# A four-layer decoder step on one core: two more pairs by seven products, two pairs of weight sums made later, norms and a decode store moved

## The chip, the cores and the metric

The kernel runs on one core of a Trainium2 chip. The time is the device time of one execution in microseconds (us). Three executions took 2382.0, 2383.22 and 2391.43 us, with a median of 2383.22 us. The engines are named as in the profile: PE is TensorE, DVE is VectorE, ACT is ScalarE, POOL is GpSimd, SP is SyncE. SP and POOL issue the transfers.

## The reference

The reference is one inference step of a small decoder with 1024 prompt positions, eight single-token samples and a model width of 2048. Its core, cut:

```python
def pool_layer(x, prefix, pos, w_in, w_grp, scale, w_out, g_ln, b_ln):
    z = x @ w_in
    u, gate = z[..., :D_POOL], z[..., D_POOL:]
    d, new_state = multiscale_pool(u, prefix, pos)        # trailing windows 2, 4, 8, 16
    d = jnp.einsum('btgc,gce->btge', d.reshape(B, T, N_POOL_GROUPS, POOL_GROUP), w_grp)
    d = d.reshape(B, T, D_POOL) * scale
    y = (d * jax.nn.silu(gate)) @ w_out
    return layer_norm(ALPHA * x + y, g_ln, b_ln), new_state

def attn_layer(x, pos, kb, vb, k_pos, q_pos, blocked, w_in, sinks, w_out, g_ln, b_ln):
    z = x @ w_in
    q = rope_partial(z[..., :D_ATTN].reshape(B, T, N_HEADS, HEAD_DIM), pos)
    gate = z[..., D_ATTN:]
    o = attn_core(q, kb, vb, q_pos, k_pos, sinks).reshape(B, T, D_ATTN)   # window 128, sinks
    y = (o * jax.nn.silu(gate)) @ w_out
    return layer_norm(ALPHA * x + y, g_ln, b_ln)
```

One pool layer runs first, then the shared keys and values (`w_kv`) are projected from its output, then one attention layer. Everything is float32. The matrices that matter are called `wia` (into the pool layer), `woa` (out of it), `wkv`, `wib` (queries and gates of the attention layer) and `wob` (out of it, the last matrix).

## The kernel before

**Chunks and stages.** The positions are cut into chunk 0 (512 positions) and chunk 1 (512 and the eight samples, 520). The stages stand in `PHASES`, an order written by hand: pool-layer input of chunk 0 (stage one, in a plain part and a part by seven products) and of chunk 1 (two), its output matrix for both chunks (three and four), attention input of chunk 0 (five, again in two parts) and of chunk 1 (six), and the last matrix for chunk 0 (seven) and chunk 1 (eight).

**Exact products in halves.** Each float32 operand is split into a rounded high half (a cast on ACT, L464 for weights, L742 for activations) and the rest (a difference on DVE, L479 and L751). A block of weights times a tile is then three matmuls: high by high, high by low, low by high (L631, L632, L633 in the seven-product form, L659, L660, L661 in the plain form). Every third matmul needs the difference.

**Eight or seven products.** Weights come in pairs of 128-column blocks, cut into four quarter blocks of 128 x 1024. In the plain form (`unit`) four blocks meet 512 positions each: for one pair two units of 48 matmuls with 512 columns. In the seven-product form (`pair` and `seven`, a Strassen scheme) seven blocks, three of them as they are and four of them sums, meet seven half-width tiles, three as they are and four sums: 7 x 24 = 168 matmuls with 256 (or 260) columns. The sums of activations are made by DVE (`t_ops`, L799 to L802) in a background generator (`t_gen`) and stored in `Td`. The sums of weights are made the first time that a pair is met, by `plain_pair` (L275, with its stores at L276 on POOL) or by `first_pair` (L328, stores at L329 on POOL), and loaded again by `next_pair` for the second chunk. For the output matrices a generator, `sum_gen`, makes them ahead of time: for each pair four parts of 256 columns, each with two loads at L405 (SP), three additions at L412, L416 and L417 (DVE) and a store at L418 (POOL). Then both chunks use `next_pair`.

**Stage five.** A step `p` is a pair of query blocks and a pair of gate blocks, and with them the attention of two heads pairs `t` in small matmuls between the others: scores (L1517), a transposition (L1570), values (L1594). A query is rotated before its scores (`q_done`: products at L1382, a sum at L1489, with data swapped between partitions by transfers at L1374). Before, steps 0 to 3 are plain and steps 4 to 7 go by seven products.

**Background work.** `end` runs after each block's matmuls (a plain unit has four such ends, a seven-product pair seven). It takes one step of the generator at the head of `side` whenever `int(i / every)` grows and enough slots are free, and one of `extra` (`sum_gen` of `wob`). In the plain part of stage five `side` holds the norm of chunk 1 after the pool layer (`ln_gen`, L848 to L927, whose output goes through `t_ops` as well) and the `t_gen` of chunk 0. In stage eight it holds the last norm of chunk 0 (`ln_gen`, L884 to L927). A stage that needs a generator's result forces its remaining steps (`ready`, `sums`).

**Order and memory.** PE, DVE and ACT run in the order of the source (`in_order`), so an instruction that waits holds all behind it on its engine. SP and POOL also issue in their order. Almost all tiles live in 53 slots (`Mem`), each of 1040 floats per partition, handed out by age of release. A tile that takes over a slot waits for the last readers of the one before, transfers too.

**The decode.** In stage six, after the gates of steps 3 and 7, `decode` attends the eight samples for half of the heads; its second half runs on into stage seven. Its steps `s0` to `s9` share one half slot `W`. The last, `s9` (L1735 to L1743), multiplies the values by the gate (kept in `sgd`, one tile for each half) and stores the result to `act["o", 1]` on SP (L1741).

Of the kernel before, what the change touches and what calls it, by code (L numbers as in the profile page):

```python
# [47 lines left out]
N_CST = 384 + 4 * NST  # L48

PHASES = (  # L50
    ("ai", 0, (0, 1)), ("ai", 0, (1, 4)), ("ai", 1, (0, 4)), ("ao", 0, None), ("ao", 1, None), ("bi", 0, (0, 4)),
    ("bi", 0, (4, 8)), ("bi", 1, (0, 8)), ("bo", 0, None), ("bo", 1, None),
)
PHASE_OF = {"x": "ai", "g": "ao", "h": "bi", "o": "bo"}
INPUT_OF = {k: x for x, k in PHASE_OF.items()}
# [13 lines left out]
    (5, 0), (5, 2), (5, 1), (6, 0), (5, 3), (5, 4), (6, 2), (6, 1), (7, 0), (6, 3), (7, 2), (7, 1), (6, 4),  # L69
    (7, 3), (7, 4), (5, 5), (5, 6), (6, 5), (6, 6), (7, 5), (7, 6),  # L70
)
X_KEEP = 5
X_AGE = 3
SIDE_KEEP = 5
# [105 lines left out]
class Kern:  # L180
# [174 lines left out]
    def build_stream(self):  # L355
        io = self.io
        w = []
        for kind, c, part in PHASES:
            seven, locked = (kind, c, part) not in PLAIN, (kind, c) in LOCKED
            pr = (lambda name, q: self.next_pairs(name, [q], False)) if seven else self.plain_pair  # L360
            if seven and c == 0:
                pr = lambda name, q: (lambda f: [f[i] for i in ORDER7])(self.first_pair(name, q))
            if kind == "ai":
                for g in range(*part):
                    for q in (2 * g, 2 * g + 1, 8 + 2 * g, 9 + 2 * g):
                        w += pr("wia", q)
                    for h in range(2):
                        w.append(self.lone(io["wg"][g][:, h * 1024 : (h + 1) * 1024]))
            elif kind == "bi":
                if part[0] == 0:  # L370
                    w += self.next_pairs("wkv", range(2), locked) if seven else pr("wkv", 0) + pr("wkv", 1)
                if seven:
                    for p in range(*part):
                        w += pr("wib", p) + pr("wib", 8 + p)
                else:
                    for p in range(*part):
                        q, g = pr("wib", p), pr("wib", 8 + p)
                        w += q[:2] + g[:2] + q[2:] + g[2:]
            else:
                name = "woa" if kind == "ao" else "wob"  # L380
                if (kind, c, part) != PHASES[-1]:
                    w += self.next_pairs(name, range(8), locked)
                    continue
                w += self.next_pairs(name, range(SPLIT[0]), locked)
                late = {q: self.next_pair(name, q) for q in SPLIT}
                w += [late[q][i] for q, i in TAIL]
        self.stream = w
        self.loaded = self.made = self.cast = self.prepped = 0
        self.hl, self.late = {}, []

    def sum_gen(self, name):


        W = 256
        parts = [(q, slice(W * h, W * h + W)) for q in range(8) for h in range(4)]
        w = self.io[name]
        held = {}

# [8 lines left out]
        def add(n):  # L407
            q, cs = parts[n]
            s = held[n]
            t = s.v(4, W)  # L410
            add = self.nc.vector.tensor_add
            add(t[:, 0:2, :], t[:, 0:2, :], t[:, 1:3, :])  # L412
            if name == "wob" and self.hurry is not name:
                yield
            held.pop(n)
            add(t[:, 2, :], t[:, 2, :], t[:, 0, :])  # L416
            add(t[:, 3, :], t[:, 3, :], t[:, 2, :])  # L417
            self.nc.gpsimd.dma_start(self.ws[name][q][:, :, cs], t)  # L418
            s.free(True)
            if n % 4 == 3:  # L420
                self.summed[name] = q + 1

        if name == "wob":

# [1232 lines left out]
    def decode(self, c, pr):  # L1657
# [4 lines left out]
        x = {}  # L1662
# [70 lines left out]
                    )  # L1733

        def s9():  # L1735
            a3 = a[:, :64].rearrange("p (t b) -> p t b", t=8)
            nc.vector.scalar_tensor_tensor(
                a3, x["p"][:, :64].rearrange("p (b t) -> p t b", t=8), 0.5, self.sgd[pr][:],
                op0=ALU.mult, op1=ALU.mult,
            )  # L1740
            nc.sync.dma_start(self.act["o", c][:, 8 * pr : 8 * pr + 8, TP:], a3)  # L1741
            x["v"].free(True)
            W.free()  # L1743

        for n, go in zip(DEC_AT[pr], (s0, s1, s2, s3, s4, s5, s6, s7, s8, s9)):
# [109 lines left out]
    def run(self):  # L1855
# [15 lines left out]
        for n, (kind, c, part) in enumerate(PHASES):  # L1871
# [36 lines left out]
            elif (kind, c) == ("bi", 0) and not self.strassen:  # L1908
                self.summed["wob"] = 0
                self.extra = self.sum_gen("wob")  # L1910
                for k in (4, 40):
                    self.at(k, lambda k=k: setattr(self, "on", k == 4))
                add(("h", 1, False), self.ln_gen(1, *acc[1], C_GA, C_BA, self.act["h", 1], self.Td.get(("h", 1))))
                add(("h", 0, False), self.t_gen(("h", 0)))

                for k in range(10):
                    self.at(2 * k + 3, lambda: self.side and self.lastO < self.i - 1 and self.side_step())
                self.every = 1.2
            elif (kind, c) == ("bi", 1):
                self.at(8, lambda: setattr(self, "on", True))  # L1920
                self.every, self.room = 1, 0
            elif (kind, c) == ("bo", 0):
                self.at(23, lambda: setattr(self, "ahead", (7, 4, 3)))
                self.at(18, lambda: add(("o", 1, False), self.t_gen(("o", 1))))
                self.at(16, lambda: [s.free() for s in self.kv])
                self.rt.free()
            elif (kind, c) == ("bo", 1):
                gen = self.ln_gen(0, *acc[0], C_GB, C_BB, io["y0"], None)
                self.at(3, lambda gen=gen: add("y", gen))
                self.every = 2  # L1930
            if kind == "ai":
                self.phase_ai(c, range(*part), nxt)
            elif kind == "bi":
# [149 lines left out]
```

## Time and profile before

| what | value |
| --- | --- |
| median of three runs | 2383.22 us |
| profiled execution, its own time | 2385.67 us |
| its span, from first to last instruction | 2383.9 us |
| PE busy | 2332.1 us (98%) |
| DVE busy | 1921.6 us (81%) |
| ACT busy | 1336.0 us (56%) |
| mean granted PE clock | 0.994 |
| stage five, plain part | about 1086 to 1347 us |
| stage five by seven products | about 1347 to 1550 us |
| stage six | about 1550 to 2005 us |
| stage seven | about 2005 to 2186 us |
| stage eight | about 2186 to 2360 us, and then the last norm to 2384 us |

A row of a table of stretches gives the stretch, its length, the busy time and the number of instructions of PE, weight loads (PEld), DVE, ACT and POOL, the clock that PE was granted as a share of its full speed, the share of the DMA engines' time and GB/s; with a filter by line, the busy times are of that line alone. A row of waits gives who waited for whom, the total in us, how often, and the longest. A row of the timeline gives start, length, engine, line, what was done, and in brackets how long the engine was idle before it and who released it. Matmuls overlap in a pipeline, so their own lengths are longer than the distance between their starts.

### The profile page before, as it was taken

The numbers are of one execution on the slowest core, as the hardware profiler recorded it, in microseconds if no ns is written. First come the engines' busy times: TensorE is split into PE (matmuls) and PEld (weight loads), VectorE is DVE, ScalarE is ACT, GpSimd is POOL, SyncE is SP. The second block draws the span as 40 slices with busy tenths as digits, with TensorE's granted clock in tenths as the row PEclk, the third lists the DMA queues.
The fourth block names the chain that finished last, engine by engine and source line by source line (L and its number), as shares of the span: only waits on it lengthen the run. The fifth ranks groups of instructions, "written<-read, shape, count | busy, mean of one in ns | idle before, by whom it ended". The sixth has DMA issues, their size and how long they took to land. (4 is left out here: it accounts for less than half of the span.)

```text
span 2383.9 us, 46511 instructions
## 1 busy us (share of the span) xinstructions
PE 2332.1 (98%) x18402; PEld 2220.6 (93%) x18402; DVE 1921.6 (81%) x2389; ACT 1336.0 (56%) x2411; POOL 196.5 (8%) x369
## 2 busy tenths in 40 slices
PE   8999999999999999999999999999999999999996
PEld 6899999999999999998788899999999999999996
DVE  8787988776878768958997888887776678789877
ACT  4444446444546546644545656675666578556655
POOL 0111110000000000001121111100000000000000
PEclk9999999999999999999999999999999999999998
DMA  8678889888989888989998776888776679799884
GB/s 292 217 247 296 282 284 363 310 307 302 296 301 347 311 274 315 349 291 327 320 359 302 250 234 217 275 275 277 240 244 220 212 234 317 217 334 375 298 276 145
DMA packets 258155, 675.38 MB, mean 283 GB/s; under 512 B 25872, under 2 KB 112656, under 8 KB 257936
## 3 DMA queue, kind: packets, MB, share of 16 engines
q1 hardware_dynamic: 212464, 507.33, 64.6%
q0 software_dynamic: 45472, 165.07, 17.7%
q8 instruction: 144, 2.36, 0.4%
q14 instruction: 75, 0.61, 0.1%
HBM read 477.23 MB, written 185.56 MB: 278 GB/s over the span
## 5 line engine op out<-in xcount | busy, mean ns | idle before, releaser
L631 PE MATMUL pD<-m,m 128*128 128x260 f32 (+1 forms) x4752 | 1350.1, 284 | 11.3 <-ACT pD L572 4.4
L633 PE MATMUL pD<-m,m 128*128 128x260 f32 (+1 forms) x4752 | 1341.8, 282 | 5.9 <-DVE m L479 5.8
L632 PE MATMUL pD<-m,m 128*128 128x260 f32 (+1 forms) x4752 | 1341.2, 282 | 0.0
L631 PEld LDWEIGHTS pD<-m,m 128*128 128x128 f32 x4752 | 896.8, 189 | 23.5 <-issue 15.6
L633 PEld LDWEIGHTS pD<-m,m 128*128 128x128 f32 x4752 | 897.2, 189 | 7.5 <-DVE m L479 7.3
L479 DVE TENSOR_TENSOR m<-m,m 128x1024 fp32r<-128x1024 f32 x674 | 814.7, 1220 | 108.7 <-ACT m L464 59.4
L632 PEld LDWEIGHTS pD<-m,m 128*128 128x128 f32 x4752 | 896.8, 189 | 1.7 <-issue 1.4
L464 ACT CAST m<-m 128x1024 fp32r<-128x1024 f32 x674 | 701.2, 1048 | 307.9 <-DVE m L328 69.5
L659 PE MATMUL pD<-m,m 128*128 128x512 f32 x448 | 180.3, 402 | 8.0 <-ACT m L742 8.0
L660 PE MATMUL pD<-m,m 128*128 128x512 f32 x448 | 177.5, 396 | 1.1 <-DVE m L751 1.1
L661 PE MATMUL pD<-m,m 128*128 128x512 f32 x448 | 177.1, 395 | 0.0
L751 DVE TENSOR_TENSOR m<-m,m 128x1024 fp32r<-128x1024 f32 (+1 forms) x120 | 147.1, 1227 | 6.4 <-ACT m L742 5.9
L604 ACT COPY m<-pD 128x260 f32<-128x260 f32 (+1 forms) x83 | 31.0, 374 | 195.4 <-PE pD L633 195.0
L742 ACT CAST m<-m 128x1024 fp32r<-128x1024 f32 (+1 forms) x120 | 125.8, 1053 | 14.3 <-PE pD L660 5.2
L659 PEld LDWEIGHTS pD<-m,m 128*128 128x128 f32 x448 | 84.8, 189 | 30.3 <-ACT m L742 8.0
L592 DVE TENSOR_TENSOR m<-pD,m 128x260 f32<-128x260 f32 (+1 forms) x86 | 36.5, 424 | 85.5 <-PE pD L633 85.3
L660 PEld LDWEIGHTS pD<-m,m 128*128 128x128 f32 x448 | 84.9, 189 | 21.0 <-DVE m L751 2.2
L661 PEld LDWEIGHTS pD<-m,m 128*128 128x128 f32 x448 | 84.8, 189 | 20.0
L328 DVE TENSOR_TENSOR m<-m,m 128x1024 f32<-128x1024 f32 x80 | 97.8, 1223 | 6.3 <-DMA m<-in_wia 2.7
L1553 ACT ACTIVATE m<-m,sm 128x128 f32<-128x128 f32 x256 | 99.2, 389 | 0.0
L1015 PE MATMUL pD<-m,m 128*128 128x260 f32 (+1 forms) x528 | 91.5, 323 | 0.0
L1015 PEld LDWEIGHTS pD<-m,m 128*128 128x128 f32 x528 | 79.5, 188 | 8.2
(197 smaller groups left out, 2118.7 us busy)
## 6 DMA issues: line engine op xcount, KB each, us to landing
m<-in_wia SPq DMA_DIRECT2D x124, 512.0 KB, 6.7
m<-in_wib SPq DMA_DIRECT2D x120, 512.0 KB, 5.8
swia<-m POOLq DMA_DIRECT2D x64, 512.0 KB, 4.6
m<-swia SPq DMA_DIRECT2D x64, 512.0 KB, 6.5
m<-swoa SPq DMA_DIRECT2D x64, 512.0 KB, 6.7
swib<-m POOLq DMA_DIRECT2D x64, 512.0 KB, 5.5
m<-swib SPq DMA_DIRECT2D x64, 512.0 KB, 5.3
m<-swob SPq DMA_DIRECT2D x64, 512.0 KB, 6.4
```

The source lines that it names most:

```text
L464: self.nc.scalar.copy(hi.r[:, :1024], self.stream[self.cast].src().a[:, :1024])
L479: self.nc.vector.tensor_sub(lo.r[:, :1024], s.src().a[:, :1024], hi.a[:, :1024])
L631: nc.tensor.matmul(ps[:, :TH], wh[:, s], h, start=new and k == 0, stop=False, skip_group_check=on)
L632: nc.tensor.matmul(ps[:, :TH], wh[:, s], l, start=False, stop=False, skip_group_check=on)
L633: nc.tensor.matmul(ps[:, :TH], wl[:, s], h, start=False, stop=k == 7, skip_group_check=on)
L659: nc.tensor.matmul(ps[:], wh[:, s], h, start=par == 0 and k == 0, stop=False)
L660: nc.tensor.matmul(ps[:], wh[:, s], l, start=False, stop=False)
L661: nc.tensor.matmul(ps[:], wl[:, s], h, start=False, stop=par == 1 and k == 7)
L742: self.nc.scalar.copy(h.r[:, :n], s.a[:, :n])
L751: self.nc.vector.tensor_sub(l.r[:, :n], s.a[:, :n], h.a[:, :n])
L1015: nc.tensor.matmul(ps[:, : cs.stop - cs.start], ws[:, s], d[:, cs], start=f0 and k == 0, stop=l0 and k == 3,)
L1553: nc.scalar.activation(x["s3"][:, i, :], x["s3"][:, i, :], AF.Exp, bias=nm[:, i : i + 1], scale=0.125, accum_out=rs[:, i : i + 1],)
```

## The change

Five things change.

- Stage five's plain part holds steps 0 to 2 and not 0 to 3; step 3, two pairs, goes by seven products. Its weights are then met by `first_pair` and not `plain_pair`.
- Pairs 2 and 3 of the last matrix (`LATE`) are left out of `sum_gen`. In stage seven they come through `first_pair`, which makes their sums there, and stage eight loads the stored sums as before.
- `sum_gen` may start new parts from step 4 to step 24 of the plain part, not to step 40.
- The background work of the plain part runs at every step (`every` 1, not 1.2), that of stage eight, the last norm of chunk 0, at every third and not every second.
- The decode's last step writes its result over the gate in `sgd` and stores it from there; the half slot `W` is no longer the source of a transfer, and the slot of the values is released as one that no transfer reads.

```diff
-    ("ai", 0, (0, 1)), ("ai", 0, (1, 4)), ("ai", 1, (0, 4)), ("ao", 0, None), ("ao", 1, None), ("bi", 0, (0, 4)),
-    ("bi", 0, (4, 8)), ("bi", 1, (0, 8)), ("bo", 0, None), ("bo", 1, None),
+    ("ai", 0, (0, 1)), ("ai", 0, (1, 4)), ("ai", 1, (0, 4)), ("ao", 0, None), ("ao", 1, None), ("bi", 0, (0, 3)),
+    ("bi", 0, (3, 8)), ("bi", 1, (0, 8)), ("bo", 0, None), ("bo", 1, None),
...
+LATE = (2, 3)
...
                 if (kind, c, part) != PHASES[-1]:
-                    w += self.next_pairs(name, range(8), locked)
+                    prs = [self.next_pair(name, q) for q in range(8)]
+                    if (kind, c) == ("bo", 0):
+                        for q in LATE:
+                            prs[q] = self.first_pair(name, q)
+                    w += [pr[i] for i in ORDERL for pr in prs[:2]]
+                    w += [pr[i] for pr in prs[2:] for i in ORDER7]
                     continue
...
-        parts = [(q, slice(W * h, W * h + W)) for q in range(8) for h in range(4)]
+        qs = [q for q in range(8) if name != "wob" or q not in LATE]
+        parts = [(q, slice(W * h, W * h + W)) for q in qs for h in range(4)]
...
             if n % 4 == 3:
-                self.summed[name] = q + 1
+                self.summed[name] = min([p for p in qs if p > q], default=8)
...
         def s9():
-            a3 = a[:, :64].rearrange("p (t b) -> p t b", t=8)
+            a3 = self.sgd[pr][:]
             nc.vector.scalar_tensor_tensor(
-                a3, x["p"][:, :64].rearrange("p (b t) -> p t b", t=8), 0.5, self.sgd[pr][:],
+                a3, x["p"][:, :64].rearrange("p (b t) -> p t b", t=8), 0.5, a3,
                 op0=ALU.mult, op1=ALU.mult,
             )
             nc.sync.dma_start(self.act["o", c][:, 8 * pr : 8 * pr + 8, TP:], a3)
-            x["v"].free(True)
+            x["v"].free()
             W.free()
...
-                for k in (4, 40):
+                for k in (4, 24):
                     self.at(k, lambda k=k: setattr(self, "on", k == 4))
...
-                self.every = 1.2
+                self.every = 1
...
                 gen = self.ln_gen(0, *acc[0], C_GB, C_BB, io["y0"], None)
                 self.at(3, lambda gen=gen: add("y", gen))
-                self.every = 2
+                self.every = 3
```

## The prediction

> **What bounds the kernel now.** I read the page first, then the busy time by stage, then the waits of TensorE (PE), and from there the places.
>
> ```profile
> span 2383.9 us, 46511 instructions
> PE 2332.1 (98%) x18402; PEld 2220.6 (93%) x18402; DVE 1921.6 (81%) x2389; ACT 1336.0 (56%) x2411; POOL 196.5 (8%) x369
> ```
>
> ```profile
> 1086.00:1347.00 261.00, 259.11 (x1306) 208.12 (x1305) 225.51 (x305) 130.93 (x285) 44.96 (x84) 0.99 0.88 313
> 1347.00:1550.00 203.00, 199.91 (x1789) 192.83 (x1788) 176.64 (x203) 134.81 (x309) 24.15 (x48) 0.99 0.74 244
> 2005.00:2186.00 181.00, 177.96 (x1560) 173.85 (x1559) 148.01 (x181) 110.36 (x183) 9.09 (x17) 1.00 0.89 305
> 2186.00:2360.00 174.00, 170.52 (x1375) 167.07 (x1373) 145.21 (x156) 100.08 (x142) 2.67 (x5) 1.00 0.78 270
> ```
>
> The stretches of the second fence are the plain part of stage five (kv and four steps by eight products), its seven-product part, stage seven and stage eight; the columns are PE, weight loads, VectorE (DVE), ScalarE, POOL, then PE's granted clock, DMA share and GB/s. PE is busy nearly all the time, so fewer matmul columns shorten the run. But DVE is at 86%, 87%, 82% and 83% there, in order, and when it is late PE stops:
>
> ```profile
> PE pD L633 <- DVE m L479: 5.8, 5, 3.0
> PE pS L1517 <- DVE m L1489: 2.5, 2, 1.9
> ```
>
> L479 makes the low half of a weight block, needed by every third matmul; L1489 ends the rotation of a query, needed by its scores. So each edit has two prices, PE's own time and what DVE does just before something PE needs.
>
> **The change part by part.**
>
> *One step of stage five by seven products.* A step is a query pair and a gate pair, 192 matmuls of 512 columns or 336 of 256, with two heads' attention inside in either form. Two windows hold exactly one steady step each (64 of the 192 are at L659, 112 of the 336 at L631):
>
> ```profile
> 1237.20:1291.90 54.70, 25.85 (x64) 12.00 (x65) 1.00 0.98 353
> 1452.68:1502.18 49.50, 31.77 (x112) 21.09 (x113) 1.00 0.68 223
> ```
>
> 54.7 - 49.5 = 5.2 us less, a few tenths either way for the windows' edges. In the changed program the passage from eight to seven products has the same instructions on DVE and ScalarE as before, eight weight blocks earlier, so I keep what is lost there.
>
> *The price in the plain part.* The norm of the second chunk (L884 to L927, with the sums of L799 to L802) and the Td transform of the first have 16 loop steps fewer to fit in (every 1.2 becomes 1), so they stand closer together; the early sums of the last matrix run to step 24 there, not 40, which takes four of their parts out. What stands ahead of the first two query rotations I counted in the order of the two programs, from the first weight block of the stage on. Ahead of the first: two L927 and two sets of L799 to L802 more. Ahead of the second: two L927 and three sets more, two L412 and one pair L416, L417 less.
>
> ```profile
> 1140.00:1182.00 42.00, 42.00 (x190) 33.78 (x189) 40.74 (x60) 22.22 (x43) 7.89 (x14) 1.00 0.91 323
> 1158.42 0.69 DVE L1489 TENSOR_TENSOR m<-m,m 128x512 f32<-128x512 f32 x1
> 1162.50 0.70 PE L1517 MATMUL pS<-m,m 64*128 64x256 f32 x4
> 1183.77 0.69 DVE L412 TENSOR_TENSOR m<-m 128x512 f32<-128x512 f32 x1 [1.58 <-DMA m<-in_wob]
> 1184.38 1.23 DVE L927 TENSOR_TENSOR m<-m,m 128x1040 f32<-128x1040 f32 x1
> 1185.53 1.22 DVE L479 TENSOR_TENSOR m<-m,m 128x1024 fp32r<-128x1024 f32 x1
> 1187.99 0.69 DVE L1489 TENSOR_TENSOR m<-m,m 128x512 f32<-128x512 f32 x1
> 1188.60 0.42 DVE L416 TENSOR_TENSOR m<-m 128x256 f32<-128x256 f32 x1
> 1189.40 0.42 DVE L799 TENSOR_TENSOR m<-m 128x260 f32<-128x260 f32 x1
> 1190.88 0.68 DVE L1635 SCALAR_TENSOR_TENSOR m<-m,m 128x512 f32<-128x512 f32 x1
> 1188.83 0.70 PE L1517 MATMUL pS<-m,m 64*128 64x256 f32 x4 [1.89 <-DVE m L1489]
> ```
>
> DVE has no slack here (40.74 of 42). From start to start an L927 takes 1.15 us (1184.38 to 1185.53), a set 1.48 (1189.40 to 1190.88), L412 0.61, the pair 0.80 (1188.60 to 1189.40). So the first rotation ends 2 x 1.15 + 2 x 1.48 = 5.3 us later, against a slack of 1162.50 - 1159.11 = 3.4: a stall of up to 1.9. The second ends 2.3 + 4.4 - 1.2 - 0.8 = 4.7 later, or 3.1 if the 1.58 us for a load goes with the L412 behind it; its scores already wait 1.89. Both stalls together then reach 1.9 + 3.1 to 1.9 + 4.7, that is 3.1 to 4.7 more. PE's clock falls after such a stop:
>
> ```profile
> 1188.00:1192.00 4.00, 3.17 (x18) 0.76 0.98 271
> 1192.00:1196.00 4.00, 4.00 (x16) 0.82 0.98 393
> ```
>
> That is 4 x 0.24 + 4 x 0.18 = 1.7 us, paid already; a second stop could add as much. I take +4.5, near the upper end because a second drop of the clock is likely; ends 0 (waits of DVE elsewhere absorb it) and +8 (4.7, 1.7 of clock and one more load late by 1.6, as the transfers, at 0.98 of capacity in the last two rows, are packed closer too). After the stop DVE has caught up.
>
> [...]
>
> *The decode store from its own tile.* Before, the gated decode output lies in a half slot W that is freed while its store (L1741, SP queue) still runs, and the next weight difference gets that slot:
>
> ```profile
> 1847.35 0.37 SPq L1741 DMA_DIRECT2D o<-m  x1
> 1852.11 2.54 DVE L479 TENSOR_TENSOR m<-m,m 128x1024 fp32r<-128x1024 f32 x2 [4.78 <-DMA o<-m]
> PE pD L633 <- DVE m L479: 3.0, 1, 3.0
> 1850.00:1854.00 4.00, 0.97 (x6) 0.78 0.48 132
> 1854.00:1858.00 4.00, 4.00 (x20) 0.50 0.00 0
> 1858.00:1862.00 4.00, 4.00 (x32) 0.87 0.52 115
> ```
>
> After, it is written over the gate in sgd, which nothing else takes, and the L479 in that place waits in the program for its own load and cast only. DVE's 4.78 us go, and with them 3.0 idle on PE (3.03 of the window's 4) and 4 x 0.50 + 4 x 0.13 = 2.5 of clock: -5.5, ends -7.3 (4.78 and 2.5) and 0 (another transfer becomes the late one). The store stays on SP and waits for the same instruction; what is queued behind it is not held longer. The other slots of the decode come free earlier than before, after PE's last read: nothing. At the second decode, in stage seven, no such wait shows: nothing.
>
> *Two pairs of the last matrix summed in stage seven.* Eight of the 32 parts of the early sums go: 8 x (L412, L416, L417), about 6 us of DVE in the seven-product part and the two stages after it, with 16 loads and 8 stores. In stage seven the two pairs load five blocks instead of seven, make four sums each (8 of L328) and store them (8 on POOL, which sits idle for most of the stage).
>
> ```profile
> L328 DVE TENSOR_TENSOR m<-m,m 128x1024 f32<-128x1024 f32 x80 | 97.8, 1223 | 6.3 <-DMA m<-in_wia 2.7
> DVE m L1208 <- ACT m L1204: 3.4, 1, 3.4
> DVE m L592 <- PE pD L633: 3.3, 2, 1.9
> DVE m L1164 <- ACT m L604: 1.7, 1, 1.7
> PE pD L633 <- DVE m L479: 0.5, 1, 0.5
> m<-swob SPq DMA_DIRECT2D x64, 512.0 KB, 6.4
> ```
>
> The waits are those between 2050 and 2100 us, where the sums come to stand; PE's shows that weight differences are barely in time there. The last row is the landing of a load. 8 x 1.22 = 9.8 us of new work meets 3.4 + 3.3 + 1.7 = 8.4 us in which DVE waits for others. The order shows two sums ahead of the L1208, one ahead of an L597, two ahead of an L1164, which fill those waits; the rest falls right before weight differences. The sums of other stages waited 6.3 / 80 = 0.08 us each for their loads. I take +2 us, between -1 (the relief just before) and +7 (most of the 9.8 on the path). The 6 us that DVE is spared before count for nothing more: the stops named here are the only ones of any length.
>
> *The last norm of chunk 0 at every third step.* Two stretches of stage eight:
>
> ```profile
> 2260.00:2280.00 20.00, 17.64 (x144) 17.19 (x143) 18.43 (x18) 11.87 (x17) 0.00 (x0) 1.00 0.97 362
> 2280.00:2300.00 20.00, 20.00 (x169) 20.00 (x168) 13.68 (x14) 9.61 (x15) 0.53 (x1) 1.00 0.85 293
> PE pD L631 <- DVE m L592: 1.2, 1, 1.2
> PE pD L633 <- DVE m L479: 1.1, 1, 1.1
> PE pD L631 <- ACT m L918: 0.6, 1, 0.6
> ```
>
> The waits (2236 to 2284 us) are 2.9 us, where L926 and L927 crowd DVE; the order puts up to 6 to 8 us of them later, behind 2280, where DVE has 6 of 20 us free. The same number of output stores leaves on SP, later, and the last set is done before the split tail's last seven products. -2.9, ends -2.9 and +2.4 (an L926 and an L927 of the tail right before something that PE needs).
>
> The sum: -5.2 + 4.5 - 5.5 + 2.0 - 2.9 = -7.1. The profiled execution took 2385.67 us, 1.8 beyond its span, and would take 2378.6. The median of the runs shown is 2383.22, 2.4 below it, so the forecast is 2376.
>
> **The rivals.**
> *Scores not later.* DVE's waits ahead of the rotations (one of 1.58 is above) absorb the added sets. For it: 225.51 of 261 leaves DVE waits somewhere. Against it: 40.74 of 42. Then the 4.5 falls to about 0: 2371.5.
> *The decode wait finds a successor.* Slots are handed out anew from the first changed allocation on, and another slot whose transfer runs may come up there. Against it: the waits of the program at that place. 2376 + 5.5 = 2381.5.
> *DVE becomes the bound in stage seven* (the other side). The eight sums come where weight differences are barely in time; if the two blocks of a pair's first sum land late, that sum holds all of DVE. It decides once these loads are issued less than a landing of 6.4 us ahead: 9.8 on the path and 6.4 twice for the loads, less the 2 counted: 2376 + 20.6 = 2396.6, and half of it, 2386, when one pair is late. Against it: 0.08 us per sum elsewhere.
> *The seven products bring nothing*, because DVE holds stage five: its 225.51 us in the plain part fall by about the moved step's share only. Against it: PE filled both windows of a step. Then -5.2 falls away: 2381.
>
> **How the numbers follow.** Forecast with its small terms (2372 to 2380): 0.54. Scores not later, alone or with a cheap stage seven: 0.20, about half of it below 2371.3. Successor: 0.09. Seven products bring nothing: 0.08. DVE the bound in stage seven: 0.09, half of it above 2395. The range 2369 to 2386 leaves out some 0.15. A measurement of this kernel tells about 0.5%, 11.9 us, from no change. Faster than 2371.3: 0.10 from the second case and 0.10 from the lower end of the first, with some of the error that I cannot name: 0.24; slower than 2395.1: 0.06; the rest 0.70.
>
> **What would show it.** Right: a stretch of 49.5 us with 112 of the seven-product matmuls in place of one of 54.7; the waits for L1489 at the scores 5 us or more in total; no wait of DVE for the store of o at the first decode, and the clock at 1.00 there; 96 of L328 (80, 8 for stage five and 8 for stage seven) with a few tenths of DMA wait each at most; no wait of PE around the last norm. Wrong: a first score without a stop, a wait of L479 for some transfer near the decode, waits of L328 for in_wob above 2 us, or PE waits in stage eight moved into its tail.

## The result, and the profile after

The changed kernel took 2377.75 us (median of 19 runs, 2373.59 to 2383.44) beside 2383.32 us (19 runs, 2380.24 to 2391.43) of the kernel before on the same chips: a ratio of 0.9975, with a 95% interval from 0.9969 to 0.9982. That is some 6 us, and half of the 0.5% that the prediction named as its bound for a difference. The profiled execution took 2377.71 us, so it stands where the median does, while the profiled one of before stood 2.4 us above its median. The two profiles are therefore 8.0 us apart, 2.4 us more than the medians. Lines of the changed kernel stand 8 lower from L479 on (L479 is now L487, L631 is L639, L1489 is L1497, L1517 is L1525) and 2 lower around L269 to L328.

From the page after, the span and the busy time of the engines:

```profile
span 2375.9 us, 46757 instructions
PE 2323.4 (98%) x18546; PEld 2221.2 (93%) x18546; DVE 1927.1 (81%) x2379; ACT 1342.7 (57%) x2422; POOL 194.9 (8%) x369
```

PE is busy 8.7 us less (2332.1 before) and DVE 5.5 more (1921.6). Where the 8.0 us went is seen step by step. The first six steps of stage five, as stretches from the first matmul of a step to that of the next (columns: stretch, length, then busy time and instructions of PE, weight loads, DVE, ScalarE and POOL, then PE's clock, DMA share, GB/s), first of the kernel before:

```profile
1131.90:1181.20 49.30, 49.30 (x225) 39.79 (x224) 48.04 (x67) 25.12 (x48) 8.61 (x15) 1.00 0.89 314
1181.20:1237.30 56.10, 54.21 (x273) 43.32 (x272) 48.72 (x76) 32.49 (x80) 10.85 (x20) 0.97 0.99 367
1237.30:1292.00 54.70, 54.70 (x305) 43.78 (x304) 46.21 (x77) 26.33 (x69) 10.77 (x21) 1.00 0.98 354
1292.00:1346.70 54.70, 54.70 (x305) 43.72 (x304) 42.95 (x51) 29.33 (x69) 8.45 (x17) 1.00 0.64 217
1346.70:1402.80 56.10, 53.41 (x483) 51.21 (x482) 49.31 (x58) 33.99 (x68) 7.01 (x14) 0.97 0.70 225
1402.80:1449.90 47.10, 47.08 (x411) 45.52 (x410) 39.97 (x45) 31.47 (x78) 5.70 (x12) 1.00 0.73 238
```

And of the changed kernel:

```profile
1131.60:1182.80 51.20, 49.55 (x226) 39.80 (x225) 49.98 (x72) 28.42 (x53) 9.62 (x18) 1.00 0.92 330
1182.80:1237.80 55.00, 52.58 (x273) 42.28 (x272) 48.67 (x86) 28.06 (x71) 10.92 (x22) 1.00 0.99 363
1237.80:1298.20 60.40, 56.37 (x305) 44.72 (x304) 46.08 (x56) 30.98 (x74) 9.24 (x19) 0.97 0.79 281
1298.20:1354.30 56.10, 53.48 (x481) 51.30 (x480) 49.31 (x58) 34.04 (x68) 7.02 (x14) 0.97 0.69 224
1354.30:1401.30 47.00, 46.94 (x411) 45.37 (x410) 40.00 (x45) 31.57 (x78) 5.69 (x12) 1.00 0.72 237
1401.30:1451.00 49.70, 49.64 (x451) 48.02 (x450) 43.00 (x51) 32.49 (x79) 6.37 (x13) 1.00 0.68 223
```

The fourth row is now the first step by seven products (56.1, as before's fifth row), and the moved step does save what it should: rows four to six take 152.8 us in place of 157.9, 5.1 less. But rows one to three, plain in both, take 166.6 in place of 160.1, 6.5 more. The third, which was a clean 54.7, is 60.4. So stage five lost 1.4 us over these six steps. The gain came later. Taken the same way, the fifth to seventh step of stage six (the first decode is among them) went from 161.7 to 154.5 (-7.2), stage seven from 180.5 to 180.0, stage eight with its tail from 198.4 to 196.6; with -0.3 ahead of the steps and +0.4 in the last two of stage five that makes -8.0.

Where PE waited in stage five of the changed kernel (who waited for whom, total, times, longest), and, from the timeline of SP, ScalarE and DVE, what went before the longest of these waits:

```profile
PE pS L1525 <- DVE m L1497: 6.4, 2, 4.0
PE pD L639 <- ACT m L1561: 2.6, 1, 2.6
PE pO L844 <- DVE m L905: 1.7, 1, 1.7
```

```profile
1226.01 0.59 ACT L1782 COPY m<-pD 128x512 f32<-128x512 f32 x1 [4.94 <-PE pD L669]
1226.58 0.37 SPq L740 DMA_DIRECT2D m<-h  x1
1231.12 0.34 SPq L271 DMA_DIRECT2D m<-in_wib  x1
1231.57 0.43 SPq L740 DMA_DIRECT2D m<-h  x1
1232.10 2.58 SPq L1382 DMA_DIRECT2D m<-m  x4
DMA to landing us min/median/max: 13.6/14.2/14.8
1240.85 1.22 DVE L487 TENSOR_TENSOR m<-m,m 128x1024 fp32r<-128x1024 f32 x1
1247.68 1.29 DVE L1390 TENSOR_TENSOR m<-m,m 128x512 f32<-128x512 f32 x2 [5.61 <-DMA m<-m]
1249.00 0.69 DVE L1497 TENSOR_TENSOR m<-m,m 128x512 f32<-128x512 f32 x1
SPq L271 <- DMA th<-m: 4.1, 1, 4.1
```

To rotate a query, four small transfers (L1382) first swap its partition groups into a second tile. The query was out of PE's accumulator at 1226.6 (L1782), but these transfers were issued only from 1232.10 on: SP was held for 4.1 us by the weight load ahead of them (L271), whose slot was still being stored. Issued at last, they landed 13.6 to 14.8 us later. DVE stood 5.61 us for them and PE 4.0. In the kernel before, the same four were issued at 1226.1 to 1229.2 and landed after 5.4 to 6.1 us:

```profile
1226.15 4.05 SPq L1374 DMA_DIRECT2D m<-m  x4
DMA to landing us min/median/max: 5.4/5.8/6.1
```

What is new in front of and among them are the loads of h and Td (L740) for the part by seven products: the activations for that part are opened at the third-last query of the plain part, and that is now one step earlier. The kernel before has the same crossing one step later, with a smaller price:

```profile
1269.16 0.38 SPq L732 DMA_DIRECT2D m<-h  x1
1284.76 2.44 SPq L1374 DMA_DIRECT2D m<-m  x4
DMA to landing us min/median/max: 8.2/8.7/9.2
1294.89 1.29 DVE L1382 TENSOR_TENSOR m<-m,m 128x512 f32<-128x512 f32 x2 [2.02 <-DMA m<-m]
1280.00:1300.00 20.00, 20.00 (x115) 16.00 (x115) 11.26 (x18) 14.03 (x35) 2.13 (x4) 1.00 0.93 317
```

There the swap was waited for too, but only by DVE and for 2.02 us, and PE was busy for all of these 20 us. The query was out at 1280.8, the swap was issued 3.9 us later and landed after 8.2 to 9.2 us; in the changed kernel these are 5.5 us and 13.6 to 14.8 us.

Around that stop and after it, and around the decode of stage six (store of its output, the weight difference behind it, and two stretches), the changed kernel shows:

```profile
1246.00:1250.00 4.00, 0.25 (x2) 0.25 (x4) 2.29 (x4) 3.60 (x7) 0.00 (x0) 1.00 1.06 361
1250.00:1254.00 4.00, 4.00 (x20) 2.87 (x19) 3.97 (x8) 3.36 (x6) 1.40 (x3) 0.62 1.07 379
1254.00:1258.00 4.00, 4.00 (x18) 3.20 (x18) 3.90 (x6) 0.00 (x0) 0.00 (x0) 0.95 0.77 299
```

```profile
1849.40 0.37 SPq L1749 DMA_DIRECT2D o<-sgd  x1
1849.29 2.49 DVE L487 TENSOR_TENSOR m<-m,m 128x1024 fp32r<-128x1024 f32 x2
1850.00:1854.00 4.00, 4.00 (x36) 4.00 (x35) 3.95 (x5) 3.98 (x13) 0.00 (x0) 1.00 0.65 165
1854.00:1858.00 4.00, 4.00 (x36) 4.00 (x35) 2.96 (x7) 3.39 (x13) 0.71 (x1) 1.00 0.78 237
```

The stop cost 4.0 us and 4 x 0.38 + 4 x 0.05 = 1.7 us of clock. At the decode, the store now leaves from its own tile, the two differences follow the gating without a gap (4.78 us before), and PE is busy all the time at full clock.

### The profile page after: what moved, and what is told of

It is laid out like the page before. It is cut to its first block, busy times and chain, and to the rows that moved or that the text cites. A ratio compares the mean times of both kernels' runs of the same rounds, so it can differ in the third digit from the quotient of the medians.

```text
span 2375.9 us, 46757 instructions
## 1 busy us (share of the span) xinstructions
PE 2323.4 (98%) x18546; PEld 2221.2 (93%) x18546; DVE 1927.1 (81%) x2379; ACT 1342.7 (57%) x2422; POOL 194.9 (8%) x369
## 5 line engine op out<-in xcount | busy, mean ns | idle before, releaser
L639 PE MATMUL pD<-m,m 128*128 128x260 f32 (+1 forms) x4864 | 1380.7, 284 | 9.2 <-ACT pD L580 3.5
L641 PE MATMUL pD<-m,m 128*128 128x260 f32 (+1 forms) x4864 | 1371.3, 282 | 2.2 <-DVE m L487 2.2
L640 PE MATMUL pD<-m,m 128*128 128x260 f32 (+1 forms) x4864 | 1371.2, 282 | 0.0
L639 PEld LDWEIGHTS pD<-m,m 128*128 128x128 f32 x4864 | 916.4, 188 | 22.0 <-issue 12.3
L487 DVE TENSOR_TENSOR m<-m,m 128x1024 fp32r<-128x1024 f32 x680 | 821.6, 1219 | 102.2 <-ACT m L472 62.7
L667 PE MATMUL pD<-m,m 128*128 128x512 f32 x384 | 154.3, 402 | 8.0 <-ACT m L750 8.0
L668 PE MATMUL pD<-m,m 128*128 128x512 f32 x384 | 152.0, 396 | 1.2 <-DVE m L759 1.2
L669 PE MATMUL pD<-m,m 128*128 128x512 f32 x384 | 151.8, 395 | 0.0
L330 DVE TENSOR_TENSOR m<-m,m 128x1024 f32<-128x1024 f32 x96 | 117.3, 1222 | 4.7 <-DMA m<-in_wia 3.1
L600 DVE TENSOR_TENSOR m<-pD,m 128x260 f32<-128x260 f32 (+1 forms) x88 | 37.3, 423 | 87.4 <-PE pD L641 87.0
L1023 PE MATMUL pD<-m,m 128*128 128x260 f32 (+1 forms) x528 | 91.5, 323 | 0.0
```

Source lines behind the costliest of these rows:

```text
L330: self.nc.vector.tensor_add(s[out].a[:, :1024], s[x].a[:, :1024], s[y].a[:, :1024])
L487: self.nc.vector.tensor_sub(lo.r[:, :1024], s.src().a[:, :1024], hi.a[:, :1024])
L639: nc.tensor.matmul(ps[:, :TH], wh[:, s], h, start=new and k == 0, stop=False, skip_group_check=on)
L640: nc.tensor.matmul(ps[:, :TH], wh[:, s], l, start=False, stop=False, skip_group_check=on)
L641: nc.tensor.matmul(ps[:, :TH], wl[:, s], h, start=False, stop=k == 7, skip_group_check=on)
L667: nc.tensor.matmul(ps[:], wh[:, s], h, start=par == 0 and k == 0, stop=False)
```

## The experiments

Each kernel was run beside the kernel before on the same chip; ratios are to that one, with a 95% interval. The expectations speak of two theories of the price in the plain part. Theory one is the prediction's: the norm's work, packed closer, puts more on DVE ahead of the query rotations. Theory two came from the profile above: the transfers are late. The first four runs do one part of the change each.

**The decode store alone.**

```diff
-            a3 = a[:, :64].rearrange("p (t b) -> p t b", t=8)
+            a3 = self.sgd[pr][:]
...
-            x["v"].free(True)
+            x["v"].free()
```

> The kernel before with the decode store from its own tile alone. The prediction's sum: 5.5 us faster (3.0 of wait and 2.5 of clock), a ratio of 0.9977, and no wait of VectorE for the store of o at the first decode. The rival (a successor takes the wait's place): 0 to 2 us faster, with another wait of L479 for a transfer within 30 us of that place. From the two profiles, where the step and its neighbours got 7 us shorter: up to 7 us.

Measured: 0.9988 (0.9979 to 0.9996), 2378.32 us, so -2.9 us (-5.0 to -1.0). In its profile stage six takes 450.0 us, not 455.5: the step with the decode goes from 56.8 to 50.2, and 1.0 of it is lost in the step ahead of that one. Both profiles give the predicted 5.5 at the place; the whole time gives less, and 5.5 lies outside its interval. In the profile of this run part of the rest is seen: stage five begins at 1087.6 us in place of 1085.6. Of these 2.0 us, 4 x 0.12 + 4 x 0.31 = 1.7 are a drop of PE's clock (0.88 from 360 to 364 us and 0.69 from 364 to 368), where the kernel before has 1.00, though the longest stop ahead of it is 2.2 us in both. That the medians differ for this reason is not shown.

**The two pairs summed in stage seven alone.**

```diff
-        parts = [(q, slice(W * h, W * h + W)) for q in range(8) for h in range(4)]
+        qs = [q for q in range(8) if name != "wob" or q not in LATE]
+        parts = [(q, slice(W * h, W * h + W)) for q in qs for h in range(4)]
```

> The kernel before with pairs 2 and 3 of the last matrix summed in stage seven, alone. The prediction's sum: 2 us slower (ratio 1.0008). If VectorE's waits for others take up all of the eight sums, and the spared early sums give a little: 0 to 1 us faster. If VectorE becomes the bound there: 10 us slower and more.

Measured: 1.0011 (1.0002 to 1.0019), 2384.49 us, +2.5. The two pairs take 27.5 and 20.6 us in place of 26.0 and 19.9, which is +2.2 and what was reckoned; the seventh step of stage six goes from 51.3 to 50.1 in return.

**The last norm at every third step alone.**

```diff
-                self.every = 2
+                self.every = 3
```

> The kernel before with the last norm of chunk 0 at every third step, alone. The prediction's sum: 2.9 us faster (ratio 0.9988), no wait of PE for L479, L592 or L918 around the norm. Rival, that the tail pays: 0 to 1 us faster, with new waits behind the first three quarters of stage eight.

Measured: 0.9989 (0.998 to 0.9998), 2379.34 us, -2.6. Stage eight with its tail takes 195.3 us, not 198.4, and of the 2.9 us of waits there one of 0.6 is left, beside the 1.4 or 1.5 us in the tail that all profiles have. As forecast.

**The moved step alone,** with its denser norms and its shorter window for the early sums.

```diff
-    ("bi", 0, (0, 4)), ("bi", 0, (4, 8)),
+    ("bi", 0, (0, 3)), ("bi", 0, (3, 8)),
...
-                for k in (4, 40):
+                for k in (4, 24):
...
-                self.every = 1.2
+                self.every = 1
```

> The kernel before with the moved step alone (with it the background work at every step and the early sums from step 4 to 24). Theory one, VectorE's order, as in the prediction: 5.2 us gained, 4.5 lost at the scores of the first two rotations, 0.7 us faster. Theory two, transfers: the forced transform and the loads fill the DMA engines, the partition swap of a later rotation lands 5 us late, and PE stops there for 4 us and more: 0.5 to 2 us slower, with VectorE's L1382 waiting 5 us for a transfer near 1247 us.

Measured: 1.0038 (1.0025 to 1.005), 2391.61 us (5 runs), some 9 us slower. The part that was to bring the most makes the kernel slower by itself. Its stage five has the steps of the changed kernel almost to the tenth (51.2, 55.0, 60.8, 56.0, 47.0, 49.7). Its profiled execution took 2387.8 us, the fastest of the five, so part of the 9 us is not in that profile.

**The whole change without the moved step.**

```diff
-    ("bi", 0, (0, 3)), ("bi", 0, (3, 8)),
+    ("bi", 0, (0, 4)), ("bi", 0, (4, 8)),
...
-                for k in (4, 24):
+                for k in (4, 40):
...
-                self.every = 1
+                self.every = 1.2
```

> The changed kernel with four steps plain again (background work at every 1.2 and early sums to step 40 as before); decode store, sums in stage seven and norm stay changed. Theory one (VectorE's order at the first two scores, step worth 0.7 us): 0.7 us slower than the changed kernel, 4.9 us faster than before (ratio 0.998). Theory two (transfers; the step costs 1.5 us): 1.5 us faster than the changed kernel, 7 us faster than before (ratio 0.997).

Measured: 0.9963 (0.995 to 0.9975), 2374.84 us, about 3 us faster than the changed kernel. Stage five takes 460.3 us, against 465.9 in the changed kernel. The intervals of the two ratios overlap (0.995 to 0.9975, and 0.9969 to 0.9982), but the run before this one lies clear of the kernel before, and both point the same way: the step moved to the seven products costs time.

**The partition swaps issued on ScalarE's queue,** everywhere in the changed kernel.

```diff
-            self.nc.sync.dma_start(t.a[32 * a : ...], s.a[32 * b : ...])
+            self.nc.scalar.dma_start(t.a[32 * a : ...], s.a[32 * b : ...])
```

> The changed kernel with the partition swaps of the rotations issued on ScalarE's queue and not on SP's, behind the loads. Theory one (VectorE's order): the swaps are not what is late, so the stops at the scores stay at 6 us and the time at the changed kernel's within 1 us, or above it by what ScalarE loses to issuing. Theory two (transfers): the swap of the fourth rotation no longer lands 12 us after its issue, the stop of 4.0 us at its scores and 1.7 of clock go: 4 to 6 us faster than the changed kernel.

Measured: 1.008 (1.0067 to 1.0094), 2401.79 us, 24 us slower than the changed kernel. The total refutes what was expected, but the place confirms it. The first line below is the landing of the four transfers of the fourth rotation in this run; the other two are ScalarE's group at L580, in this run and then in the changed kernel.

```profile
DMA to landing us min/median/max: 5.9/6.9/8.0
L580 ACT ACTIVATE pD<-pD 128x260 f32<-128x260 f32 (+1 forms) x86 | 31.7, 369 | 99.0 <-PE pD L641 72.7 <-issue 12.6 <-DMA m<-in_wkv 6.7
```

```profile
L580 ACT ACTIVATE pD<-pD 128x260 f32<-128x260 f32 (+1 forms) x86 | 31.7, 368 | 73.7 <-PE pD L641 73.2
```

Four sets of the Td transform still stand in a row on DVE (1232.7 to 1238.6; 1228.9 to 1234.8 in the changed kernel), and the DMA share there is still 1.03 to 1.04, yet the transfers land in 5.9 to 8.0 us, not 13.6 to 14.8, the fourth rotation waits for nothing, and the third step takes 55.4 us, not 60.4. So neither the row of sets nor the full DMA engines by themselves stopped the scores, but the place of the swaps behind the loads on SP's queue. The price is elsewhere: the swaps now stand in ScalarE's own order, right ahead of its copies from one accumulator to another (L580). These wait 25 us more than before, and PE waits 18.6 us for them (3.5 in the changed kernel). Why the transfers land sooner from ScalarE's queue than from SP's, this run does not show.

**The early sums begun only with stage six, and the early sums of the plain part without their additions.**

```diff
-                for k in (4, 24):
-                    self.at(k, lambda k=k: setattr(self, "on", k == 4))
...
-                self.at(8, lambda: setattr(self, "on", True))
+                self.at(0, lambda: setattr(self, "on", True))
```

> The changed kernel with no early sum of the last matrix in the plain part; they begin with stage six. Four parts go from there: 7 us of VectorE and 4 MB of transfers. Both theories: the stop at the second scores (2.4 us) goes. Theory two: that at the fourth (4.0 and 1.7 of clock) shrinks as well, 4 to 6 us faster than the changed kernel; theory one: 2 to 3 us faster. Either way up to 3 us may be lost where stage seven then forces the last sums.

```diff
+            plain = name == "wob" and not self.strassen
+            if plain:
+                add = lambda *_: None
             add(t[:, 0:2, :], t[:, 0:2, :], t[:, 1:3, :])
```

> The changed kernel without the additions of the early sums in the plain part; their loads and stores stay, so pairs 0 of the last matrix are stored as they were loaded and the result is not the reference's. VectorE has 7 us less there, the transfers are the same. Theory one: the stops at the scores go, 3 to 5 us faster than the changed kernel. Theory two: the stop at the fourth scores stays at about 4 us, and at most the 2.4 us at the second go.

Measured: 0.9987 (0.9978 to 0.9995), 2379.81 us, and 0.9966 (0.9953 to 0.9978), 2375.82 us. Both take the load off the first two steps (49.2 and 52.6 us; 49.4 and 53.6). Neither brings the third back to 54.7: it takes 61.9 and 59.2 us, with stops of 4.5 and 2.8 at the fourth scores. So the early sums press the first two rotations, as theory one has it, and the largest stop stands without them, though it is 1.2 us shorter in the second run. Moved to stage six the sums are paid there: its steps take 454.0 us, 5.9 more than in the changed kernel, and the first of the two runs is 2 us slower than that kernel, where every expectation had it faster.

**The activations opened one query later.** This one line decides when the loads of h and Td for the part by seven products may begin.

```diff
-                if t == 2 * ps[-1] - 1:
+                if t == 2 * ps[-1]:
                     self.x_begin(nxt)
```

> The changed kernel with one line other: in the plain part of stage five the loading of the activations for the seven-product part is opened one query later (at t = 4, not t = 3). Theory two in its second form (the fourth rotation is late because that opening forces three sets of the Td transform onto DVE in a row and puts the loads of h and Td ahead of and among the partition-swap transfers, which land 14.2 us after their issue): the third step falls from 60.4 to 55 or 56 us, the wait of the fourth scores (4.0) goes, and the time is 4 to 6 us below the changed kernel's, a ratio of 0.995 to 0.996 to the kernel before. Theory one (two more norm steps and the closer packing ahead of the rotations cost it): the third step stays above 59 us and the ratio at 0.9975. A third way: the activations land too late for the first step by seven products, which then waits at L639 for a weight or activation, and the time is above the changed kernel's.

Measured: 0.9972 (0.9963 to 0.9981), 2374.47 us. In its profile, the swaps of the fourth rotation with their landing, then the third and fourth step:

```profile
1226.06 3.18 SPq L1382 DMA_DIRECT2D m<-m  x4
DMA to landing us min/median/max: 8.6/9.3/9.3
1237.30:1291.90 54.60, 54.60 (x305) 43.73 (x304) 44.72 (x58) 29.57 (x72) 8.96 (x18) 1.00 0.88 306
1291.90:1350.30 58.40, 54.44 (x482) 52.27 (x481) 50.51 (x59) 35.41 (x69) 7.10 (x14) 0.94 0.68 238
PE pD L639 <- ACT m L1561: 4.0, 1, 4.0
```

The swaps are issued 6 us earlier, the third step is 54.6 us, and the stop is gone with its drop of the clock, as theory two has it. Of these 5.8 us, 2.3 come back in the next step: the first by seven products takes 58.4 us, where PE waits 4.0 us for ScalarE's exponentials (2.6 in the changed kernel) and loses 58.4 x 0.06 = 3.5 us of clock (56.1 x 0.03 = 1.7 there). In all the run is 3.3 us faster than the changed kernel by the medians and 0.7 us by the ratios, short of the 4 to 6 that were expected; the intervals overlap, so the gain in the whole time is not shown.

**The decode store and the norm together, and the moved step with the two late pairs.**

```diff
+            a3 = self.sgd[pr][:]
...
+                self.every = 3
```

> The kernel before with two edits alone: the decode store from its own tile and the last norm at every third step; four plain steps and all eight pairs summed early. If the parts add up: -3 and -2.7 from the two runs of one part, so 2376.5 and a ratio of 0.9977, and the sums of two pairs in stage seven would then have been worth a gain of 2 us in the run with all but the moved step (0.9963). If those sums cost their 2 us there too, the two edits together bring 8 to 10 us: 2372 to 2374, a ratio of 0.996 to 0.9955. The stretch of stage five is a copy of the kernel before and takes 460 to 464 us as in the other profiles.

```diff
+    ("bi", 0, (0, 3)), ("bi", 0, (3, 8)),
...
+LATE = (2, 3)
```

> The kernel before with the moved step (with its closer packing) and the two pairs of the last matrix summed in stage seven, without the decode store and the norm. The moved step alone took 1.0038 times the kernel before, and it costs about 3 us within the whole change. If the two edits belong together, since the eight parts left out are those that the shorter window leaves over for the seven-product part: 2 to 5 us above the kernel before, a ratio of 1.001 to 1.002. If they only add up: 1.0038 and 1.0011, a ratio of 1.0049, 11 to 12 us above.

Measured: 0.9972 (0.9963 to 0.9981), 2375.41 us, and 1.0034 (1.0021 to 1.0046), 2389.17 us. The two edits add up to the -5.5 of their single runs within the interval, and they alone are already as fast as the whole change. The moved step with the late pairs costs 8 us (5 to 11), where the two single runs give +11.7 and the idea that the two belong together gave +2 to +5: it lies between them, and tells them apart only weakly. What it does show is the step's cost a second time: the late pairs without the step took 1.0011 (1.0002 to 1.0019), and the two intervals do not touch.

**The later opening, with the norms at the old pace.**

```diff
-                self.every = 1
+                self.every = 1.2
```

> The run with the later opening of the activation loads, and in it the second norm and the Td transform of the plain part again at every 1.2 loop steps as in the kernel before, not at every step. It tells apart the two places of the price. If the closer packing costs what it was reckoned to ahead of the first two rotations: the first step falls from 51.2 to 49.3 us and the second from 55.0 to 53 or 54, the wait of the second scores (2.4) goes, the third step stays at 54.7, and the time is 2 to 4 us below the run before it, 2370 to 2372.5, a ratio of 0.995 to 0.996. If the packing was needed, since the transform then is not done when the opening comes: its sets are forced in a row before the opening, the scores of the fourth or fifth query wait again, and the third step goes to 57 us or more, with no gain in all.

Measured: 0.9965 (0.9951 to 0.9978), 2374.18 us. The first step is 49.3 us and the second 52.6, where the wait for the norm's statistics and that of the second scores are gone, 4.3 us less than with the closer packing. Starting the early sums in stage six had taken away as much (4.4 us) with the packing left in: the two press together, and relieving either is enough. The third stays at 54.6. But the first step by seven products now takes 60.5 us. The wait that was 4.0 is 3.0 now (at L600), and ahead of it, at the very start of the step, PE stands for the softmax weights (L1587):

```profile
PE pD L639 <- DVE m L600: 3.0, 1, 3.0
PE pO L1602 <- ACT m L1587: 2.8, 1, 2.8
1292.00:1296.00 4.00, 1.06 (x16) 0.82 (x18) 2.48 (x3) 4.00 (x8) 0.07 (x1) 1.00 1.06 403
1296.00:1300.00 4.00, 4.00 (x33) 3.67 (x30) 3.97 (x6) 3.97 (x9) 0.00 (x0) 0.58 0.85 340
```

Of 4.3 us gained 2.1 went there; by the medians nothing can be told. Four versions beat both kernels by their medians: without the moved step (2374.84), this one (2374.18), the later opening (2374.47) and the two edits alone (2375.41). The intervals of their ratios overlap with each other and with that of the changed kernel, so none of them is shown to be the best, nor any one of them, taken alone, to be faster than the changed kernel.

## Why the prediction was right or wrong

The total came out within 2 us of the forecast, in part by luck: two groups of terms were off in opposite directions.

*The moved step, -5.2:* right. Rows four to six of the two tables give -5.1, and the passage from eight to seven products cost the same as before (56.1 us in both, with a drop of the clock in both), as assumed. Profiles with four plain steps and no drop there have 54.4 to 54.9 (last section), so against those profiles rows four to six gain 3.4 to 3.9.

*The price in the plain part, +4.5:* too small, and put in the wrong place. It was 6.5 by the two profiles. The prediction had a first stop of up to 1.9 at the first scores: there was none, though the first step did take 1.9 more, of which 1.7 stand as a wait at the norm's statistics (L844 for L905, near 1137 us), a wait that was not named. The first rotation did come 4.3 us later (L1497 at 1162.7, L1489 at 1158.4), near the 5.3 that were counted, but PE had stood before it and reached the scores 1.5 later itself. The second rotation, counted as 3.1 to 4.7 later, came 2.1 later (1190.07 and 1187.99), and the wait of its scores went from 1.89 to 2.42, with no second drop of the clock and without the one that the kernel before has there. So over both places the stops grew by 2.2, not by 3.1 to 4.7.

The failed sentence is “After the stop DVE has caught up.” At the fourth scores stood the largest stop of all, 4.0 us and 1.7 of clock, and its cause was not DVE's work but a transfer. The prediction counted instructions of DVE ahead of the rotations and gave the transfers half a sentence, in the upper end of this term (one more load late by 1.6). Its sign of being right, 5 us or more of waits for L1489 at the scores, came out as 6.4, but 4.0 of that stood at the fourth scores, where nothing was expected. It did not ask where the opening of the activations moves when the plain part loses a step. That the cause lies there is shown twice: with the swaps on another queue the stop went (third step 55.4), and with the opening one query later it went as well (54.6).

*Whether the step pays.* In six profiles with four plain steps (those of the kernel before, the first three single parts, the run without the moved step, and the two edits together) stage five takes 459.8 to 464.6 us, in the three with the moved step and nothing else in the plain part changed 465.9 to 466.7. With the later opening it takes 462.1, and with the old pace as well 460.2: inside the range of four plain steps, so there the step costs nothing in stage five and gains nothing that these profiles show. The rival “the seven products bring nothing” had this outcome, though not its cause: PE's 5 us were there, and were spent before. Over all runs the step costs between 3 us (the change with and without it) and 9 us (alone); why it costs more alone is not settled.

*The decode store, -5.5:* right at its place (stage six -5.5 in the run of this part alone), with a whole time of only -2.9 (-5.0 to -1.0). The rival that the wait finds a successor fell: no wait for a store shows there, and the clock is 1.00. The other 1.7 us of the changed kernel's -7.2 are mostly the next item.

*Two pairs in stage seven, +2:* right in size and place. What was not right is that the time spared on DVE before, put at 6 us (the three additions take 97.8 us before and 85.6 after, 12.2 less), counts for nothing: the seventh step of stage six takes 50.1 us in place of 51.3 (50.0 to 50.2 in every profile with these pairs but the one whose early sums all stand in stage six). Alone they cost 2.5 us, and in company (with or without them beside the decode store and the norm) no cost can be measured. DVE did not become the bound:

```profile
L330 DVE TENSOR_TENSOR m<-m,m 128x1024 f32<-128x1024 f32 x96 | 117.3, 1222 | 4.7 <-DMA m<-in_wia 3.1
PE pD L641 <- DVE m L487: 1.4, 3, 0.5
```

These are the sums (L328 before), 96 as counted, none waiting for in_wob, and PE's waits for weight differences in stage seven.

*The last norm, -2.9:* right, -2.6 (-4.8 to -0.5) alone, and in the changed kernel one wait of 0.9 is left ahead of the tail.

So the three small terms that were read from a wait with its row held to within a few tenths at their places, and the term that was reckoned from counted work was wrong in size and place. By the two profiles the errors are 2 us more price and 3 us more gain from stage six on (-9.5 in place of -6.4), and they covered each other. The ratios say the same with wider limits: everything but the moved step brought 8.8 us (the run without it, 0.9963), and the step then cost 3, where the prediction's terms give a gain of 6.4 and a gain of 0.7.

## What to carry to other kernels

When a stage loses a step, ask for every event that is set by counting back from the stage's end where it lands now, and what shares its queue there; here the preloading of the next part moved in front of a rotation's swap on SP's queue, and the four small transfers took 8 us longer to land. A transfer that something urgent needs is worth following from its source to its landing: here held 4.1 us on SP by the load ahead, then 14.2 us on the way. And run each part alone: the part with the largest computed gain was the one that cost time, and the small ones carried the result.

## What the runs showed of the hardware

The clock does not fall by the length of the stop alone. A stop of 2.42 us at the second scores of the changed kernel cost no clock, while one of 1.89 at the same place of the kernel before did (rows in the prediction). The changed kernel around 1190 us:

```profile
1190.91 2.00 PE L1525 MATMUL pS<-m,m 64*128 64x256 f32 x16 [2.42 <-DVE m L1497]
1186.00:1190.00 4.00, 2.49 (x11) 1.69 (x9) 3.97 (x8) 3.97 (x10) 0.53 (x1) 1.00 1.01 415
1190.00:1194.00 4.00, 3.09 (x21) 2.60 (x22) 3.93 (x9) 2.90 (x4) 0.54 (x1) 1.00 1.02 419
1194.00:1198.00 4.00, 4.00 (x19) 3.26 (x18) 3.86 (x8) 0.00 (x0) 0.00 (x0) 1.00 1.02 387
```

In three drops that the traces show in full the clock is 0.50 throughout: from 1190.06 to 1193.47 us of the kernel before, after that stop of 1.89 us, which is 1.7 us lost in 3.41; from 1251.00 to 1254.41 us of the changed kernel, after a stop of 4.0, again 1.7 lost in 3.41; and at the decode of the kernel before from 1852.25 to 1859.08, which is 3.4 lost in 6.83, part of it while PE stood. So the stop of 4.0 us cost no more clock than that of 1.89.

The same instructions also take different time in stage five. The kernel before and the three runs that share its program there (decode store alone, norm alone, both) took 464.1, 464.6, 460.3 and 459.8 us; the difference lies in the second step (56.1, 56.3, 53.9, 52.9) and the passage (56.1, 56.0, 54.4, 54.9), where the stop at the second scores was 1.9, 2.1, 1.3 and 0.2 us. Most of the rest is the clock: in both places it is 0.97 in the first two runs and 1.00 in the other two. At the passage the stop is 2.7, 2.7, 2.7 and 3.1 us, so stops of the same length were followed by a drop in two profiles and by none in the others; what decides it these runs do not show. So by these four profiles a step's time in a single one is good to about 2 us where a stop of this length stands in it (54.4 to 56.1 at the passage), or 3 us if the stop itself differs (52.9 to 56.3 in the second step), and the 6.5 us of price above contain such an error too: against the norm-alone and both-edits profiles the same three steps cost 8.7 and 9.7 us more.
